# Unread matrix products in a tuned encoder layer: eight instead of two in the fourth feed-forward pair, one more ahead of three groups of gate pairs, and a wider one at the start

## The chip, the core and the metric

The kernel runs on one core of one Trainium2 chip. The time is what the device takes for one execution, in microseconds (us); the figure for a kernel is the median of its runs. The engines are called by the profile's names: PE is the matrix engine (TensorE), PEld its loading of weights, DVE is VectorE, ACT is ScalarE, POOL is GpSimd, SP is the queue that starts most transfers.

## What is computed

One layer of an encoder on 512 tokens of 1024 channels, all in float32. Cut to what matters here:

```
h      = rms_norm(x, norm1_g)
proj   = h @ w_in                       # 1024 x 7680: three mixers and three gates
y_*    = pool mixer, differential attention, gated recurrence (from slices of proj)
gates  = sigmoid(gate columns of proj)  # three branches x 1024 channels
merged = sum over branches of gates * (y_branch @ w_up_branch)
x      = x + merged @ w_out
h2     = rms_norm(x, norm2_g)
gu     = h2 @ w_ffn_in                  # 1024 x (2 x 2816): gate half, up half
x      = x + (silu(gate half) * up half) @ w_ffn_out
out    = rms_norm(x, final_norm_g)
```

## The kernel before

The tokens lie in four blocks of 128, the channels in eight tiles of 128. Every float32 matrix operand is split into a high part, cast to the rounded type that PE reads at one pass, and a low part, the remainder; a product is then three matmuls: high by high, high by low, low by high. The high part is cast on ACT (`whi`, line 183; `shi`, line 300), the low part subtracted on DVE (`wlo`, line 184; `slo`, line 302). A name such as `fhi`/`flo`, `ghi`/`glo`, `h_hi`/`h_lo`, `hT_hi`/`hT_lo` in a row of the profile is such a pair of the moving operand.

`Jobs.stream` (from line 223) walks through a list of jobs, and a job's matmuls are issued in the order in which the list stands; `tc.keep_in_program_order` holds PE to it. So PE's order is written out by hand, and DVE and ACT serve it.

Two stages use a seven-product scheme for a 2 x 2 block product, which takes seven block products where the plain way takes eight. In the feed-forward input a **pair** is one tile of 128 up columns and the tile of gate columns beside it; pairs 1 to 21 run this way, one after the other, in four jobs each (`first`, `second`, `third`, `fourth`, from line 1230). In the gates of the mixers, five pairs of gate tiles run this way (`gate_pair_bodies`, from line 653): one in the pool branch, two and two in the attention branch. Each pair is seven block products of 12 matmuls, 84 matmuls in all, each with 256 moving columns. The ups (`up_job`, from line 691) are products of a branch with its up weights, 12 matmuls of 512 columns per tile, two tiles from one weight part.

The kernel holds some operands at chosen distances in memory: `pad` puts 64 or 192 bytes ahead of a tile, and `skip` in `split_w` (line 178) moves the split weights by 64 or 192 bytes inside their buffer. In the gate pairs and in the feed-forward pairs the weights of a matmul start 64 bytes after its moving operand, if addresses are counted modulo 128; in most products with 512 columns they start at the same place. The part that two ups share ahead of a group of gate pairs has `skip=64`, which sets its weights 64 bytes off (`add_ups`, with `skips`, from line 726).

An **unread product** is a matmul whose result no instruction reads. In the fourth pair, `first` ends with two of them, which take the part's first weight tile and 512 columns of the same weights as the moving operand, the second one 16 elements (64 bytes) further on. They write to the PSUM name `tp`, which has two buffers. At the start, `busy(n)` issues n unread products of the 128 x 128 identity matrix with itself.

The program's order after the mixers is: pool ups and gates, the pool gate pair, ups, two attention gate pairs, ups, two attention gate pairs, ups, the output projection, the second norm, the feed-forward input (pairs 1 to 21), the feed-forward output.

Of the kernel before, what the change touches and what calls it, by code (L numbers as in the profile page):

```python
# [12 lines left out]
F32R = mybir.dt.float32r  # L13
# [5 lines left out]
P = 128  # L19
# [57 lines left out]
def encoder_kernel(ctx: ExitStack, tc: tile.TileContext, x, norm1_g, w_in, pool_w, pool_scale,  # L77
# [3 lines left out]
    nc = tc.nc  # L81
# [3 lines left out]
    def pool(name, bufs=1, **kw):  # L85
        return tc.tile_pool(name=name, bufs=bufs, **kw)


    def mm(out_, lhsT, rhs, start, stop, chain=False):
        i = nc.tensor.matmul(out_, lhsT=lhsT, rhs=rhs, start=start, stop=stop, skip_group_check=chain)  # L90
        tc.keep_in_program_order(i)
        n = 1
        for d in rhs.shape[1:]:
            n *= d
        pipe.t += max(0.107, n * 0.0004167 + 0.002) if rhs.dtype == F32R else max(0.216, n * 0.001667 + 0.004)
# [18 lines left out]
    def bank(name, shape=(P, 512)):  # L114
        return psum.tile(list(shape), F32, name=name, bufs=2 if name == "tp" else 3)
# [8 lines left out]
    ident = const.tile([P, P], F32, name="ident")  # L124
# [142 lines left out]
    @contextmanager  # L267
    def behind(after):

        with ExitStack() as st:  # L270
            for i in after:
                st.enter_context(tc.issue_after(i))
            yield
# [45 lines left out]
    def product(ps, part, n, r, start):  # L319

        terms = [(part.hi, r[0]), (part.hi, r[1]), (part.lo, r[0])]
        for i, (w, m) in enumerate(terms):
            for k in range(KT // 2):
                mm(ps, w[:, n, k, :], m[:, k, :], start and i == 0 and k == 0,
                   i == 2 and k == KT // 2 - 1, True)
                if k % 2:
                    yield
# [94 lines left out]
    def cols_mm(ps, part, r, nk, sub=0, lo_col=0, n=512, r_lo_last=False):  # L422
        c = slice(lo_col, lo_col + n)
        ws = slice(sub * P, sub * P + P)
        terms = [(part.hi, r[0]), (part.hi, r[1]), (part.lo, r[0])]
        if r_lo_last:
            terms[1:] = terms[:0:-1]
        for i, (w, m) in enumerate(terms):
            for k in range(nk):
                mm(ps[:, c], w[:, k, ws], m[:, k, c], i == 0 and k == 0, i == 2 and k == nk - 1)  # L430
                if k % 2:
                    yield
# [56 lines left out]
    xg = st0.enter_context(pool("xg"))  # L489
# [10 lines left out]
    for b in range(NB):  # L500
# [6 lines left out]
        if b >= 1:  # L507
            c = OFF[("rq", "rf", "rb")[b - 1]]
# [16 lines left out]
    def busy(n):  # L525

        ps = bank("mm")
        for _ in range(n):
            mm(ps[:, 0:P], ident, ident, True, True)
# [10 lines left out]
            transpose(gt[:, j, :], g_cols[:, half * 4 + j:half * 4 + j + 1].to_broadcast([P, P]), ident)  # L540
        nc.vector.tensor_copy(out=g_b[:, half * 512:half * 512 + 512], in_=gt.rearrange("p a b -> p (a b)"))

    busy(5)

    class First:
        wpool = None
# [144 lines left out]
    def up_job(idx, dt, y, first, last_hl):  # L691
        def body(part):
            ps = bank("mm")
            yield from cols_mm(ps, part, y(), 4, dt % 2)
            sg = gate_sb.pop((idx, dt))
            if first:
                nc.vector.tensor_tensor(out=merged[:, dt, :], in0=ps, in1=sg, op=ALU.mult)
                return
            nc.vector.tensor_tensor(out=sg, in0=ps, in1=sg, op=ALU.mult)
            nc.vector.tensor_tensor(out=merged[:, dt, :], in0=merged[:, dt, :], in1=sg, op=ALU.add)  # L700
            if last_hl:
                hi, lo = last_hl()
                nc.scalar.copy(out=hi[:, dt, :], in_=merged[:, dt, :])
                nc.vector.tensor_tensor(out=lo[:, dt, :], in0=merged[:, dt, :],
                                        in1=hi[:, dt, :].bitcast(F32), op=ALU.subtract)
        return body
# [479 lines left out]
    def ffn_pair_evac(j, pg, pu):  # L1186
        sl = FF["t"].tile([P, S], F32, name="silu")
        nc.scalar.activation(out=sl, in_=pg, func=AF.Silu)
        nc.vector.tensor_tensor(out=hid_of(j), in0=pu, in1=sl, op=ALU.mult)

    def hid_of(j):
        return FF["hid"][j // 8][:, j % 8, :]
# [33 lines left out]
    def ffn_pair_bodies(j):  # L1226
        c = {}


        def first(part):  # L1230
            f = FF["forms"]
            c["x"], c["zy"] = bank("mm")[:, 0:256], bank("rc")
            c["u"] = FF["t"].tile([P, S], F32, name="u")
            yield from product(c["x"], part, 0, f.r11, True)
            nc.scalar.copy(out=c["u"][:, 0:256], in_=c["x"])
            yield from product(c["zy"][:, 0:256], part, 1, f.r21, True)


            if j == 4:
                w = part.hi.rearrange("p n k c -> p (n k c)")  # L1240
                for skip in (0, 16):
                    mm(bank("tp"), w[:, 0:P], w[:, skip:skip + 512], True, True)

        def second(part):
            f = FF["forms"]
            y = c["y"] = c["zy"][:, 256:]
            if j == 2:
                with behind(FF["s12_2"]):
                    ffn_pair_evac(0, *FF["first"])
            c["g"] = FF["t"].tile([P, S // 2], F32, name="g2")  # L1250
            yield from product(c["x"], part, 1, f.n2, False)
            nc.scalar.copy(out=c["u"][:, 256:], in_=c["x"])
            yield from product(y, part, 0, f.n1, True)
            FF["y1"] = (nc.scalar.copy(out=c["g"], in_=y).ins,)

        def third(part):
            f = FF["forms"]
            if j == 1:
                with behind(FF["forms_end"]):
                    pairs[2][1].chunk.add()  # L1260
            c["sl"] = FF["t"].tile([P, S], F32, name="silu")
            yield from product(c["x"], part, 0, f.d, False)
            on_dve = nc.vector.tensor_tensor(out=c["g"], in0=c["x"], in1=c["g"], op=ALU.add).ins  # L1263
            if j == 1:
                FF["g1"] = (on_dve,)
            nc.scalar.activation(out=c["sl"][:, 256:], in_=c["g"], func=AF.Silu, scale=-1.0)
            yield from product(c["y"], part, 1, f.r22, False)
            nc.vector.tensor_tensor(out=c["u"], in0=c["u"], in1=c["zy"], op=ALU.add)

        def fourth(part):  # L1270
            f = FF["forms"]
            yield from product(c["x"], part, 0, f.n4, False)
            nc.scalar.activation(out=c["sl"][:, 0:256], in_=c["x"], func=AF.Silu, scale=-1.0)
            nc.vector.tensor_tensor(out=hid_of(j), in0=c["sl"], in1=c["u"], op=ALU.mult)
            if j == FT - 1:
                for i in range(2):
                    hid_split(i)

        return first, second, third, fourth

    pair_bodies = {j: ffn_pair_bodies(j) for j in range(1, FT)}
# [25 lines left out]
    def hid_split(i):  # L1307

        if i in hid_parts or i > LAST_JOB:
            return  # L1310
        hi, lo = (LAST["ws"].tile([P, 2, S], F32R, name=n) for n in ("shi", "slo"))
        j = PLAIN[i][0]
        view = FF["hid"][j // 8][:, j % 8:j % 8 + 2, :]
        nc.scalar.copy(out=hi, in_=view)
        nc.vector.tensor_tensor(out=lo, in0=view, in1=hi.bitcast(F32), op=ALU.subtract)
        hid_parts[i] = hi, lo
# [432 lines left out]
```

## Time and profile before

| | us |
|---|---|
| three runs | 891.97, 883.51, 885.41 |
| their median | 885.41 |
| the profiled execution, its own time | 892.81 |
| the profiled execution, its span | 891.0 |
| PE busy in it | 878.2 (99%) |
| DVE busy | 658.8 (74%) |
| ACT busy | 441.2 (50%) |

The span runs from the first to the last instruction that the profile holds; the execution's own time is 1.8 us longer, for what lies around it. The profiled execution is the longest of the four. A busy share of PE tells little here: matmuls overlap, so PE counts as busy also where each one takes longer than it could. What counts is the distance from the start of one matmul to the start of the next, and the timeline view gives it: its rows merge like instructions that follow each other, with the start of the first, the time until the last has ended, and their count.

### The profile page before, as it was taken

The numbers are of one execution on the slowest core, as the hardware profiler recorded it, in microseconds if no ns is written. First come the engines' busy times: TensorE is split into PE (matmuls) and PEld (weight loads), VectorE is DVE, ScalarE is ACT, GpSimd is POOL, SyncE is SP. The second block draws the span as 40 slices with busy tenths as digits, with TensorE's granted clock in tenths as the row PEclk, the third lists the DMA queues.
The fourth block names the chain that finished last, engine by engine and source line by source line (L and its number), as shares of the span: only waits on it lengthen the run. The fifth ranks groups of instructions, "written<-read, shape, count | busy, mean of one in ns | idle before, by whom it ended". The sixth has DMA issues, their size and how long they took to land.

```text
span 891.0 us, 13788 instructions
## 1 busy us (share of the span) xinstructions
PE 878.2 (99%) x5598; PEld 792.6 (89%) x5598; DVE 658.8 (74%) x992; ACT 441.2 (50%) x695; POOL 19.2 (2%) x35
## 2 busy tenths in 40 slices
PE   8999999999999999999999999999999999999996
PEld 7989988888988888888999898899999999988785
DVE  6788664845868764897785646988887888746996
ACT  5544343435656583443455335655555555433553
POOL 1000000000000000000000000000000000000001
PEclk9999999999999999999999999999999999999998
DMA  7330113024223123222331860344334432355002
GB/s 240 95 119 24 49 48 118 24 72 142 67 85 122 48 77 125 95 95 81 117 89 48 277 170 1 93 118 123 96 95 115 123 96 95 119 189 188 2 0 95
DMA packets 109579, 88.52 MB, mean 99 GB/s; under 512 B 2742, under 2 KB 98508, under 8 KB 109388
## 3 DMA queue, kind: packets, MB, share of 16 engines
q1 hardware_dynamic: 108924, 86.59, 31.6%
q8 instruction: 44, 0.72, 0.3%
q10 hardware_dynamic: 592, 1.05, 0.3%
q14 instruction: 19, 0.16, 0.1%
HBM read 85.54 MB, written 2.10 MB: 98 GB/s over the span
## 4 chain that ended last, share of the span: by engine, by line
PE 87%; DVE 6%; DMA 4%; issue 1%; ACT 1%; POOL 0%; SPq 0%; POOLq 0%; DVEq 0%; ACTq 0%
PE mm L90 60%; PE rc L90 23%; PE tp L90 2%; PE tp L98 2%; DMA raw<-in_w_out_dram 1%; DVE wlo L184 1%; DMA raw<-in_w_in_dram 1%; DMA raw<-in_w_ffn_out_dram 1%; DMA raw<-in_w_ffn_in_dram 1%; DVE hid L354 1%; DVE x L1323 0%; DMA xin<-in_x_dram 0%; DVE flo L354 0%; ACT whi L183 0%; DVE hrow L455 0%
## 5 line engine op out<-in xcount | busy, mean ns | idle before, releaser
L183 ACT CAST whi<-raw 128x1024 fp32r<-128x1024 f32 (+1 forms) x134 | 128.8, 967 | 147.4 <-PE mm L90 101.5
L184 DVE TENSOR_TENSOR wlo<-raw,whi 128x1024 fp32r<-128x1024 f32 (+1 forms) x134 | 149.0, 1118 | 54.1 <-ACT whi L183 34.3
L90 PE MATMUL mm<-hT_hi,wlo 128*128 128x512 f32 (+1 forms) x380 | 92.4, 375 | 0.2 <-DVE wlo L184 0.2
L90 PE MATMUL mm<-hT_hi,whi 128*128 128x512 f32 (+1 forms) x380 | 91.6, 376 | 0.0
L90 PE MATMUL mm<-hT_lo,whi 128*128 128x512 f32 (+1 forms) x380 | 90.7, 375 | 0.0
L90 PEld LDWEIGHTS mm<-hT_lo,whi 128*128 128x128 f32 x380 | 66.6, 189 | 11.5
L90 PEld LDWEIGHTS mm<-hT_hi,whi 128*128 128x128 f32 x380 | 66.4, 189 | 11.7 <-ACT hT_hi L468 0.4
L90 PEld LDWEIGHTS mm<-hT_hi,wlo 128*128 128x128 f32 x380 | 66.3, 188 | 11.6 <-DVE wlo L184 0.4
L302 DVE TENSOR_TENSOR slo<-sums,shi 128x1024 fp32r<-128x1024 f32 x52 | 63.3, 1218 | 0.1
L300 ACT CAST shi<-sums 128x1024 fp32r<-128x1024 f32 x52 | 54.6, 1051 | 3.8 <-DVE sums L264 2.3
L261 DVE TENSOR_TENSOR sums<-raw 128x1024 f32<-128x1024 f32 x26 | 31.7, 1220 | 3.5 <-DMA raw<-in_w_in_dram 3.5
L854 DVE TENSOR_TENSOR kq<-kq,pyr 128x256 f32<-128x256 f32 x48 | 18.2, 421 | 18.2 <-PE rc L90 18.2
L90 PE MATMUL rc<-kq,kc 128*128 128x128 f32 x224 | 31.6, 284 | 0.0
L90 PEld LDWEIGHTS rc<-kq,kc 128*128 128x128 f32 x224 | 30.1, 191 | 1.5
L996 ACT ACTIVATE s<-s,mx 128x512 f32<-128x512 f32 x32 | 23.0, 721 | 15.6 <-DVE mx L994 15.4
L1263 DVE TENSOR_TENSOR g<-mm,g 128x256 f32<-128x256 f32 x21 | 8.9, 424 | 28.4 <-PE mm L90 28.4
L823 ACT COPY kc<-kq 128x512 f32<-128x512 f32 x28 | 18.6, 666 | 20.3 <-PE rc L90 12.6
L90 PE MATMUL mm<-fhi,shi 128*128 128x256 f32 x168 | 26.7, 281 | 0.6 <-ACT shi L300 0.6
L90 PE MATMUL mm<-fhi,slo 128*128 128x256 f32 x168 | 26.9, 282 | 0.5 <-DVE slo L302 0.5
L90 PE MATMUL mm<-flo,shi 128*128 128x256 f32 x168 | 26.6, 281 | 0.0
L90 PE MATMUL mm<-y_hi,whi 128*128 128x512 f32 x96 | 26.6, 395 | 0.0
L90 PE MATMUL mm<-y_lo,whi 128*128 128x512 f32 x96 | 26.4, 393 | 0.0
(370 smaller groups left out, 1995.0 us busy)
## 6 DMA issues: line engine op xcount, KB each, us to landing
raw<-in_w_ffn_in_dram SPq DMA_DIRECT2D x44, 512.0 KB, 5.4
raw<-in_w_in_dram SPq DMA_DIRECT2D x34, 512.0 KB, 4.2
raw<-in_w_in_dram SPq DMA_DIRECT2D x13, 1024.0 KB, 5.3
raw<-in_w_ffn_out_dram SPq DMA_DIRECT2D x7, 1024.0 KB, 5.1
raw<-in_w_out_dram SPq DMA_DIRECT2D x4, 1024.0 KB, 9.8
xin<-in_x_dram SPq DMA_DIRECT2D x4, 512.0 KB, 4.7
raw<-in_w_up_rec_dram SPq DMA_DIRECT2D x2, 1024.0 KB
raw<-in_w_up_pool_dram SPq DMA_DIRECT2D x2, 1024.0 KB, 5.0
```

What stands on the lines that cost most here:

```text
L90: i = nc.tensor.matmul(out_, lhsT=lhsT, rhs=rhs, start=start, stop=stop, skip_group_check=chain)
L98: tc.keep_in_program_order(nc.tensor.transpose(out_, in_, idn))
L183: nc.scalar.copy(out=hi, in_=view)
L184: LAST["wlo"] = nc.vector.tensor_tensor(out=lo, in0=view, in1=hi.bitcast(F32), op=ALU.subtract).ins
L261: nc.vector.tensor_tensor(out=strided(sums, 0, [[2 * half, 2], [1, half]]), in0=strided(self.raw, 0, [[3 * half, 2], [1, half]]), in1=stri ...
L300: nc.scalar.copy(out=hi, in_=view)
L302: on_dve = nc.vector.tensor_tensor(out=lo, in0=view, in1=hi.bitcast(F32), op=ALU.subtract).ins
L354: last[0] = form(**kw).ins
L823: nc.scalar.copy(out=strided(kc, 0, [[2 * n, S // (2 * n)], [n, 2], [1, n]]), in_=strided(kq, 2 * S, [[2 * n, S // (2 * n)], [S + n, 2], [ ...
L854: nc.vector.tensor_tensor(out=xv, in0=xv, in1=tv, op=ALU.mult)
L996: nc.scalar.activation(out=s, in_=s, func=AF.Exp, scale=-1.0, bias=mx[:, c:c + 1], accum_out=zz[:, i, c:c + 1])
L1263: on_dve = nc.vector.tensor_tensor(out=c["g"], in0=c["x"], in1=c["g"], op=ALU.add).ins
```

## The change

Three edits.

1. At the start, five identity products of 128 columns are replaced by eleven products of 256 columns on a new tile `probe`, which ACT fills with eight copies of the identity. The weights are taken 48 elements (192 bytes) into the tile. The tile makes its pool 4 KB per partition larger; no operand of another matmul moves.
2. After the second tile of each part of ups that has `skip=64`, one unread product repeats the last matmul of that tile into `tp`. There are three such places: ahead of the pool gate pair, ahead of the first two attention gate pairs, and ahead of the last two.
3. In the fourth feed-forward pair eight unread products stand in place of two: six with the moving operand at the weights' own start, then two with it 48 elements (192 bytes) further on, which is 64 bytes modulo 128.

```
-    busy(5)
+    probe = xg.tile([P, 1024], F32R, name="probe")
+    nc.scalar.copy(out=probe, in_=ident.rearrange("p (o c) -> p o c", o=1).to_broadcast([P, 8, P]))
+    ps = bank("mm")
+    for _ in range(11):
+        mm(ps[:, 0:256], probe[:, 48:48 + P], probe[:, 0:256], True, True)
...
         def body(part):
             ps = bank("mm")
             yield from cols_mm(ps, part, y(), 4, dt % 2)
+            if part.skip and dt % 2:
+                mm(bank("tp"), part.lo[:, 3, P:2 * P], y()[0][:, 3, :], True, True)
...
             if j == 4:
                 w = part.hi.rearrange("p n k c -> p (n k c)")
-                for skip in (0, 16):
+                for skip in (0, 0, 0, 0, 0, 0, 48, 48):
                     mm(bank("tp"), w[:, 0:P], w[:, skip:skip + 512], True, True)
```

In PE's order of the changed program, the end of the fourth pair's first job looks as follows. `rc<-h_hi,wlo` is the last matmul group of that job, the rows with `tp<-whi` are the unread products, `mm<-fhi,shi` opens the second job; what stands in brackets is what a row's instructions wait for.

```order
L90 MATMUL rc<-h_lo,whi 128x256 x4
L90 MATMUL rc<-h_hi,wlo 128x256 x4
L90 MATMUL tp<-whi 128x512 x2
L90 MATMUL tp<-whi 128x512 [waits PE_49] x6
L90 MATMUL mm<-fhi,shi 128x256 [waits Activation_49]
L90 MATMUL mm<-fhi,shi 128x256 x3
```

The row with x6 is new. `tp` has two buffers, so from the third product on each one waits for PE's own semaphore, that is until the product two places ahead of it has ended.

At the third of the three places with ups, ahead of the last two attention gate pairs, PE's order changes thus; `y_hi` and `y_lo` are the branch's output, `hT_hi` opens the gate pair.

```order
 L90 MATMUL mm<-y_lo,whi 128x512 x4
 L90 MATMUL mm<-y_hi,wlo 128x512 x4
+L90 MATMUL tp<-y_hi,wlo 128x512 [waits PE_49]
 L90 MATMUL mm<-hT_hi,whi 128x256 [waits DVE_49]
 L90 MATMUL mm<-hT_hi,whi 128x256 x3
```

One matmul is put between the last up and the first gate product; nothing else changes its place. Its wait is for the first of the three added products, which has long ended (the gate pairs start at 424, 439 and 470 us).

## The prediction

> **What bounds the kernel now.** I read the page first: the busy time of the engines, and the chain of work that ended last.
>
> ```profile
> PE 878.2 (99%) x5598; PEld 792.6 (89%) x5598; DVE 658.8 (74%) x992; ACT 441.2 (50%) x695; POOL 19.2 (2%) x35
> ...
> PE 87%; DVE 6%; DMA 4%; issue 1%; ACT 1%; POOL 0%; SPq 0%; POOLq 0%; DVEq 0%; ACTq 0%
> ```
>
> PE is the chain for 87% of the span. An edit that adds matmuls is paid in full there, and one that changes the distance between matmuls by a few ns is paid, or earned, thousands of times. So the next view is the timeline of PE alone. At the end of the output projection stand three rows of eight matmuls with 256 columns, and the row after them:
>
> ```profile
> 521.57 1.07 PE L90 MATMUL mm<-whi,m_hi 128*128 128x256 f32 x8
> 522.48 1.07 PE L90 MATMUL mm<-whi,m_lo 128*128 128x256 f32 x8
> 523.39 1.07 PE L90 MATMUL mm<-wlo,m_hi 128*128 128x256 f32 x8
> 524.29 1.08 PE L90 MATMUL mm<-whi,m_hi 128*128 128x512 f32 x4
> ```
>
> From 521.57 to 524.29 are 2.72 us for 24 matmuls: 113.3 ns from start to start. In the feed-forward input the same shape, with the same distance of 64 bytes between weights and moving operand, goes more slowly. Here is the end of the fourth pair's first job, with the two unread products, and the end of the stage:
>
> ```profile
> 594.70 0.64 PE L90 MATMUL rc<-h_hi,wlo 128*128 128x256 f32 x4
> 595.17 0.62 PE L90 MATMUL tp<-whi 128*128 128x512 f32 x2
> 595.63 0.63 PE L90 MATMUL mm<-fhi,shi 128*128 128x256 f32 x4
> ...
> 770.88 0.39 PE L90 MATMUL mm<-whi,shi 128*128 128x512 f32 x1
> ```
>
> Between 595.63 and 770.88 stand the other five products of the fourth pair and 17 whole pairs: 5 x 12 + 17 x 84 = 1488 matmuls in 175.25 us, 117.8 ns each. So there are **two paces** for one shape, 113.3 and 117.8 ns. It isn't the clock, which is granted in full in the window from 600 to 640 us (the figure behind the busy times):
>
> ```profile
> core 0: us, PE busy (x) PEld busy (x) DVE busy (x) ACT busy (x) POOL busy (x), PEclk, DMA share, GB/s
> 600.00:640.00 40.00, 40.00 (x342) 40.00 (x341) 32.89 (x41) 21.97 (x36) 0.00 (x0) 1.00 0.39 107
> ```
>
> Nor does PE wait for anyone there (40.00 of 40). What sets the pace shows a little earlier, in pair 1, where both occur within 11 us on the same operands:
>
> ```profile
> 569.31 0.73 PE L90 MATMUL mm<-fhi,whi 128*128 128x256 f32 x4
> 569.88 0.62 PE L90 MATMUL mm<-flo,whi 128*128 128x256 f32 x4
> ...
> 573.06 0.62 PE L90 MATMUL rc<-h_hi,wlo 128*128 128x256 f32 x4
> 574.32 0.74 PE L90 MATMUL mm<-fhi,shi 128*128 128x256 f32 x4 [0.64 <-ACT shi L300]
> ...
> 579.04 0.74 PE L90 MATMUL mm<-fhi,slo 128*128 128x256 f32 x4 [0.46 <-DVE slo L302]
> 579.62 0.64 PE L90 MATMUL rc<-h_hi,shi 128*128 128x256 f32 x4
> ```
>
> The row at 569.31 takes 0.73 instead of 0.63 us: PE stopped for about 0.1 us. From 569.88 to 573.06 it then ran 28 matmuls in 3.18 us, 113.6 ns each: fast. The stop at 579.04 ended in the other pace, 0.64 us for four instead of 0.62, and so it stayed for all of the stage. A stop draws the pace anew; without one it stays. That explains the three runs as well. If the stretch behind the fourth pair ran fast, it would take 1488 x 4.5 = 6.6 us less. The runs of 891.97 and 885.41 lie 6.56 apart. I read them as this stretch slow, and fast; the profiled execution, with 892.81, is a slow one, and the median of 885.41 already has it fast.
>
> **The change part by part.** The sum is made against the profiled execution, 892.81.
>
> *The fourth pair, the products themselves.* Two are there now; from 595.17 to 595.63 they take 0.46 us. Eight would take 8 x 0.227 = 1.82 us (0.227 is half of 0.46, rounded down) if none waited. But from the third on each waits until the product two places ahead has ended, and no row of before has such a wait. For its price I use how long such a product lasts, and how long PEld needs behind an end:
>
> ```profile
> L90 PE MATMUL tp<-whi x2: 389/393/397, 595.2 to 595.4; 128*128 128x512 f32 x2
> ...
>   ACT whi L183: 1.5, 1
> ...
> 574.30 1.22 DVE L302 TENSOR_TENSOR slo<-sums,shi 128x1024 fp32r<-128x1024 f32 x1
> ...
> 575.57 0.53 PEld L90 LDWEIGHTS mm<-fhi,slo 128*128 128x128 f32 x4 [0.26 <-DVE slo L302]
> ```
>
> A product ends 0.39 us after its start. DVE ended at 575.52 and the waiting load began at 575.57: 0.05 us. The stopped rows above are 0.11 us longer than their neighbours, the load that is no longer hidden. Thus the third can start 0.39 + 0.05 + 0.11 = 0.55 us after the first, where it would come after 0.45. Going on like this, numbers 3, 5 and 7 start at 0.55, 1.10 and 1.65, each even one 0.23 behind, and the eighth ends its turn at 2.11 us. So the cost lies between 1.82 - 0.46 = **1.4** (no stop) and 2.11 - 0.46 = 1.65; I take **1.6**, near the upper end, since all its parts are measured rows. Below nothing it can't be: nothing else uses PE meanwhile. Queued behind the waiting products on PE is all of the stage. ACT's cast of the next weights waits for the last of them (1.5 us once, in the rows above); it comes later by what PE comes later, and ACT is busy for 22 of 40 us.
>
> *The fourth pair, the pace behind it.* The two products of before did not turn slow into fast in this execution. Six waits of fixed length stand there now; each is a stop, and of the two stops shown above one ended fast and one slow. Here the stop is PE's own, so it should end alike in every execution. Between **-6.6 us** (all 1488 fast) and nothing I take -6.6, because this place follows a stop as the fast row at 569.88 does. That DVE could become the bound in its place is excluded: 32.9 us in 40 become 32.9 in 38.5, 85%.
>
> *Ups ahead of the gate pairs.* Three more matmuls with 512 columns, not waiting for anything recent:
>
> ```profile
> 423.07 1.10 PE L90 MATMUL mm<-y_hi,wlo 128*128 128x512 f32 x4
> 424.01 0.64 PE L90 MATMUL mm<-hT_hi,whi 128*128 128x256 f32 x4
> ```
>
> Four take 0.94 us from 423.07 to 424.01, so three cost **+0.7**. The five gate pairs run slowly now: 0.64 for four, and all their matmuls on `ghi`, from the listing by groups, last 281 ns on average, against 276 in the fast output projection (the second row, of 505 to 524 us alone):
>
> ```profile
> L90 PE MATMUL mm<-ghi,slo 128*128 128x256 f32 x40 | 6.3, 281 | 0.0
> ...
> L90 PE MATMUL mm<-whi,m_lo 128*128 128x256 f32 x58 | 8.2, 276 | 0.0
> ```
>
> Fast, their 5 x 84 = 420 matmuls would take 420 x 4.5 = 1.9 us less. The run of 883.51 is 1.9 below that of 885.41, which I read as just that. One more matmul makes the number of ups odd, so the pair is entered at another place of whatever alternates. The bounds are -1.9 and nothing; I take **-1.9**, a little likelier than not, as that run shows the fast entry to exist.
>
> *The start.* ACT gets one more cast, of 128x1024, and PE eleven products of 256 columns for ten passes of 128:
>
> ```profile
> 4.52 1.06 ACT L449 ACTIVATE hrow<-xin 128x1024 f32<-128x1024 f32 x1 [2.31 <-DMA xin<-in_x_dram]
> ...
> 6.27 1.28 PE L90 MATMUL mm<-ident 128*128 128x128 f32 x10
> ...
> 7.65 0.66 PE L98 MATMUL tp<-ident,hrow 128*128 128x128 f32 x4
> ```
>
> ACT is idle for 2.31 us ahead of 4.52, and a cast of that size takes 0.97 us on average by the page's groups: hidden, else +1. Eleven products at 0.12 are 1.3 us from 6.27, to 7.57; the transposes start at 7.65, released by DVE. Between 0 and +0.3; I take **0**.
>
> The sum: 892.8 + 1.6 - 6.6 + 0.7 - 1.9 = **886.6 us**. That is 6.2 below the profiled execution, but 1.2 above the median, whose runs need no cure in the long stretch.
>
> **The rivals.**
>
> *The stop ends in the slow pace* (0.22 with the gate pairs slow too). For it: at 579.04 a stop did just that, and the two products of before left it slow. All additions are paid, nothing is earned: 892.8 + 1.6 + 0.7 = 895.1, slower than the median by 1.1%, in every run, since a fast entry would be lost as well. The point where it decides: the first matmul behind the eighth product. With the gate pairs fast it is 893.2 (0.10).
>
> *The long stretch fast, the gate pairs slow* (0.25): 886.6 + 1.9 = 888.5. For it: an odd number of products at that distance also stood ahead of 595.63 (one), and slow came of it.
>
> *The change doesn't do what it says* (0.05). The pace might not hang on these products at all, but on the stops before them. Then the draw stays as it was, two of three runs fast, and the median only gains the additions: 885.4 + 1.6 + 0.7 = 887.7. The Trainium skill speaks for this, in "TensorE: Matmul & The Clock Gate", section "Step-by-step: what each phase is for": "Loading the next tile's weights doesn't steal SBUF read bandwidth from the running matmul." By that rule no placing of weights could alter the pace, and the same page's gap of N/2.4 + 2.5 ns gives 109.2 for 256 columns always, an estimate. The trace disagrees: 113.3 and 117.8 for one shape at full clock. With the rule the sum would be the 887.7 just worked out; without it, the forecast.
>
> *The start is late* (0.03): the cast holds up ACT's first square, or the eleven products the transposes: up to +1.0 on the forecast, 887.6.
>
> **How the numbers follow.** Forecast, both fast: 0.35, 886.6 us. Others as given, 0.25, 0.22, 0.10, 0.05, 0.03. The cases with a fast long stretch span 886.3 to 888.5, and unprofiled runs lie 0.8 lower (891.97 for 892.81) and differ somewhat: from 884.5. The slow ones go to 895.1; they hold a third, so the range must take them in: 884.5 to 895.5. About 1% is what a measurement of this kernel can tell from no change, 876.6 to 894.3 here. Faster by that needs 9 us, more than every gain together: 0.02. Slower is the case of 895.1, which lies just beyond the bound, at 0.6 of its chance: 0.14. The same: 0.84.
>
> **What will show it.** In the changed profile: eight rows of `tp<-whi`, 2.1 us long with the third 0.55 behind the first (1.8, if nothing waits); behind them four matmuls in 0.62 rather than 0.64 us, up to the 512-column products, which start some 168.6 us later rather than 175.25; a mean of 276 rather than 281 for `mm<-ghi,slo`; the transposes on `hrow` at 7.65. I'd be wrong if stops behind the fourth pair draw the pace again, since DVE has less slack at the fast pace, or if earlier stops, which differ from run to run, move the time by more than this change does.

## The result, and the profile after

The changed kernel takes **891.89 us** in the median of 17 runs (891.47 to 893.02), the kernel before 885.41 in the median of 17 runs taken beside it (883.51 to 891.97). The ratio is 1.007 [1.0057, 1.0083]: within 1% of before, but slower. It is 6.5 us above the median of before and 5.3 above the forecast of 886.6. It lies inside the forecast's range of 884.5 to 895.5, which was wide enough to hold the slow rivals too, so the time alone says nothing for the forecast's mechanism.

The page of the changed kernel, busy time of the engines and the chain of work that ended last:

```profile
span 890.1 us, 13812 instructions
PE 878.3 (99%) x5608; PEld 792.8 (89%) x5608; DVE 658.7 (74%) x992; ACT 441.8 (50%) x696; POOL 19.8 (2%) x35
PE 91%; DVE 4%; DMA 2%; issue 1%; ACT 1%; POOL 0%; SPq 0%; POOLq 0%; DVEq 0%
```

PE is busy for the same 99%, and with 10 matmuls more it is busy 0.1 us longer: the page alone shows nothing. The timeline of PE around the fourth pair does (start, length, engine, line, operation, tiles, count). It starts at the last stop ahead of the products and ends at the first product with 512 columns behind the stage:

```profile
577.95 0.74 PE L90 MATMUL mm<-fhi,slo 128*128 128x256 f32 x4 [0.47 <-DVE slo L302]
578.52 0.62 PE L90 MATMUL rc<-h_hi,shi 128*128 128x256 f32 x4
...
593.04 0.62 PE L90 MATMUL rc<-h_hi,wlo 128*128 128x256 f32 x4
593.49 2.30 PE L90 MATMUL tp<-whi 128*128 128x512 f32 x8
595.63 0.64 PE L90 MATMUL mm<-fhi,shi 128*128 128x256 f32 x4
596.10 0.64 PE L90 MATMUL mm<-flo,shi 128*128 128x256 f32 x4
...
770.88 0.40 PE L90 MATMUL mm<-whi,shi 128*128 128x512 f32 x1
```

Four matmuls take 0.62 us from 578.52 on, up to the products: the pairs were entered in the fast pace. Behind the products four take 0.64, and 595.63 to 770.88 are 175.25 us for 1488 matmuls, 117.8 ns each, to the hundredth what the profiled execution of before had. **The eight products turn the fast pace into the slow one.** The window in which the prediction read 342 matmuls of before, here for PE alone:

```profile
core 0: us, PE busy (x), PEclk, DMA share, GB/s
600.00:640.00 40.00, 40.00 (x342) 1.00 0.38 104
```

The clock is granted in full, PE waits for nobody, and the count is that of the slow trace of before. (At 117.8 ns 340 matmuls fit in 40 us, at 113.3 ns 353; the view also counts the two or three that only reach into the window. So a slow trace shows 342, a fast one 355 or 356, and that count serves as the sign of the pace from here on.)

The products take 2.14 us, from 593.49 to 595.63. The weight loads (PEld) show how they wait:

```profile
593.38 0.30 PEld L90 LDWEIGHTS tp<-whi 128*128 128x128 f32 x2
593.94 0.42 PEld L90 LDWEIGHTS tp<-whi 128*128 128x128 f32 x2 [0.26 <-PE tp L90]
```

The third load waits for PE itself: the first product ended 0.39 us after 593.49, at 593.88, and the load began 0.06 later. In the version without waits, below, each load begins as the product ahead of it starts, which here would be 593.72.

The entry of the three groups of gate pairs, again in the timeline of PE: the last 512-column product ahead of each, and the first matmuls behind it.

```profile
424.04 0.40 PE L90 MATMUL tp<-y_hi,wlo 128*128 128x512 f32 x1
424.27 0.62 PE L90 MATMUL mm<-hT_hi,whi 128*128 128x256 f32 x4
...
439.39 0.39 PE L90 MATMUL tp<-y_hi,wlo 128*128 128x512 f32 x1
439.62 0.63 PE L90 MATMUL mm<-hT_hi,whi 128*128 128x256 f32 x4
440.09 0.64 PE L90 MATMUL mm<-hT_lo,whi 128*128 128x256 f32 x4
...
470.48 0.40 PE L90 MATMUL tp<-y_hi,wlo 128*128 128x512 f32 x1
470.71 0.62 PE L90 MATMUL mm<-hT_hi,whi 128*128 128x256 f32 x4
471.17 0.62 PE L90 MATMUL mm<-hT_lo,whi 128*128 128x256 f32 x4
```

The first and the third group became fast, the second stayed slow. That is 84 + 168 = 252 of the 420 matmuls, worth 252 x 4.5 = 1.1 us. The listing by groups has it as a mean between 281 and 276:

```profile
L90 PE MATMUL mm<-ghi,slo 128*128 128x256 f32 x40 | 6.2, 278 | 0.0
```

The start, which the prediction put at no cost (the transposes on `hrow` at 7.65):

```profile
6.36 1.54 PE L90 MATMUL mm<-probe 128*128 128x256 f32 x11
7.74 0.63 PE L98 MATMUL tp<-ident,hrow 128*128 128x128 f32 x4
```

### The profile page after: what moved, and what is told of

It reads as the page before. It is cut to its first block, busy times and chain, and to the rows that moved or that the text cites. A ratio compares the mean times of both kernels' runs of the same rounds, so it can differ in the third digit from the quotient of the medians.

```text
span 890.1 us, 13812 instructions
## 1 busy us (share of the span) xinstructions
PE 878.3 (99%) x5608; PEld 792.8 (89%) x5608; DVE 658.7 (74%) x992; ACT 441.8 (50%) x696; POOL 19.8 (2%) x35
## 4 chain that ended last, share of the span: by engine, by line
PE 91%; DVE 4%; DMA 2%; issue 1%; ACT 1%; POOL 0%; SPq 0%; POOLq 0%; DVEq 0%
PE mm L90 62%; PE rc L90 25%; PE tp L90 3%; PE tp L98 2%; DMA raw<-in_w_out_dram 1%; DMA raw<-in_w_in_dram 1%; DVE wlo L184 1%; DVE hid L354 1%; DVE flo L354 1%; DMA xin<-in_x_dram 0%; DVE hrow L455 0%; DVE h_lo L472 0%; PE rc L98 0%; DVE slo L302 0%; DVE sums L261 0%
```

## The experiments

The theory, called Theory 1 in the quoted expectations and T1 here: the last products ahead of a run of 256-column matmuls set the pace of that run, and the eight as built set the slow one. T1a is the form in which the distance of the last product from what follows decides, long or short, and the waits of the eight make them end on the short one. Against it stands that the pace is drawn at the stops ahead and that the products change nothing but their own length. Medians are in us; the kernel before ran beside each batch: 885.92 for the first four experiments, 886.21 for the next four, 885.09 for the last four. Over these batches 16 of its 85 runs lie above 889.5 us and the other 69 below 887.8, with nothing between 887.7 and 890.8. The three batches ran on three chips, and the high runs of before are spread unevenly over them: 3 of 25, 12 of 31 and 1 of 29.

**Two products again, all else changed.**

```
-                for skip in (0, 0, 0, 0, 0, 0, 48, 48):
+                for skip in (0, 16):
```

> The changed kernel with the two products of before in the fourth pair instead of the eight; the additions ahead of the gate pairs and at the start stay. Theory 1 (the eight products set the slow pace): the changed profile comes to them at 113.3 ns, and two products leave a fast pace as it is, so all 1488 matmuls behind them are fast: 891.9 - 6.6 (pace) - 1.7 (six products) = 883.6 us. Theory 2 (the pace behind is not set by the products; something after them makes it slow): only the six products are saved, 890.2 us, with 117.8 ns behind them.

884.02 (883.52 to 890.97), ratio 0.9983 [0.9962, 1.0005]. So the eight products carry the loss. The profiled execution happened to be the one of 890.97. Its timeline of PE:

```profile
593.78 0.63 PE L90 MATMUL rc<-h_hi,wlo 128*128 128x256 f32 x4
594.25 0.62 PE L90 MATMUL tp<-whi 128*128 128x512 f32 x2
594.71 0.63 PE L90 MATMUL mm<-fhi,shi 128*128 128x256 f32 x4
595.18 0.63 PE L90 MATMUL mm<-flo,shi 128*128 128x256 f32 x4
```

From 593.78 to 594.25 and from 594.71 to 595.18 are 0.47 us for four matmuls, 118 ns each: slow ahead, slow behind. Two products leave the pace as they find it: slow here and in the first trace of before, fast in the second trace of before, below.

**Eight products alone, in the kernel before.**

```
-                for skip in (0, 16):
+                for skip in (0, 0, 0, 0, 0, 0, 48, 48):
```

> The kernel before with the eight products in the fourth pair as its only edit. Theory 1: slow behind them in every run, 885.4 + 6.6 + 1.7 = 893.7 us. Theory 2 (the slow pace comes of the other two edits): 885.4 + 1.7 = 887.1 us, fast behind them.

895.16 (four runs: 893.18 and 895.02 to 895.40), ratio 1.0098 [1.0074, 1.0121]. The timeline of PE, and the window of 40 us, of the execution at 893.18:

```profile
594.33 0.62 PE L90 MATMUL rc<-h_hi,wlo 128*128 128x256 f32 x4
594.78 2.30 PE L90 MATMUL tp<-whi 128*128 128x512 f32 x8
...
600.00:640.00 40.00, 40.00 (x342) 1.00 0.38 106
```

Fast ahead of the products, slow behind them, as in the changed kernel. This speaks against T1a: by the starts in this trace the last of the eight took 238 ns, a long distance, and the pace behind it is slow all the same. The three runs without a profile are 1.3 to 1.7 us above the 893.7 that T1 gives; that is not explained.

**Eight products in one buffer: no waits between them.**

```
+                t = bank("tp")
                 for skip in (0, 0, 0, 0, 0, 0, 48, 48):
-                    mm(bank("tp"), w[:, 0:P], w[:, skip:skip + 512], True, True)
+                    mm(t, w[:, 0:P], w[:, skip:skip + 512], True, True)
```

> The changed kernel with its eight products written to one buffer of tp, so that none waits for an earlier one. Theory 1a (what counts is whether the last product with 512 columns ends in the long, 236 ns, or the short, 231 ns, one of the two distances that alternate): without waits the last two should take 225 and 236 ns, the pair is entered behind a long one, and all is fast: 891.9 - 6.6 - 0.3 (no waits) = 885.0 us. Theory 1b (any such row of products resets to slow): 891.6 us.

885.17 (884.59 to 885.92), ratio 0.9991 [0.9981, 1.0001]. The same eight products, and none of ten runs is slow. The timeline of PE, and the window:

```profile
593.63 2.00 PE L90 MATMUL tp<-whi 128*128 128x512 f32 x8
595.47 0.63 PE L90 MATMUL mm<-fhi,shi 128*128 128x256 f32 x4
595.94 0.62 PE L90 MATMUL mm<-flo,shi 128*128 128x256 f32 x4
...
600.00:640.00 40.00, 40.00 (x355) 1.00 0.41 114
```

They take 1.84 us instead of 2.14, so the waits themselves cost 0.3; the lost pace costs 6.6. The edit takes away two things together, the waits and the change from one buffer to the other with each product. No run parts them; what the traces show is that the distances of 316 to 336 ns of the waiting rows are gone (226 to 234 here). In one point the text above was wrong: the last two were to take 225 and 236 ns, and took 233 and 234.

**No products in the fourth pair at all** (the block `if j == 4:` removed).

> The changed kernel without any unread product in the fourth pair. Theory 1: the pace that the first three pairs reached goes on. It is fast in the changed profile (113.3 ns from 578.6 us), so 891.9 - 6.6 - 2.1 = 883.2 us. Theory 2: slow in the long stretch, 889.8 us. If the pace that pairs 1 to 3 reach differs from run to run, the runs fall into two groups 7 us apart.

883.61 (883.09 to 890.97, one run of ten above 884.3), ratio 0.9979 [0.9954, 1.0004]. Its window shows

```profile
600.00:640.00 40.00, 40.00 (x356) 1.00 0.43 116
```

By its trace, and by the times of nine runs of ten, the long stretch is fast without any product: what the stop ahead of it leaves. So the products of the changed kernel don't fail to set the fast pace, they destroy it.

**Is it the number of products?** Two, and three, in one buffer, with both operands 64 bytes apart:

```
+                t = bank("tp")
-                for skip in (0, 0, 0, 0, 0, 0, 48, 48):
-                    mm(bank("tp"), w[:, 0:P], w[:, skip:skip + 512], True, True)
+                for skip in (48, 48):               # and (48, 48, 48)
+                    mm(t, w[:, 0:P], w[:, skip:skip + 512], True, True)
```

> The changed kernel with two products in the fourth pair, both 64 bytes off, in one buffer without a wait. Theory of the alternation (a matmul with 256 columns goes on fast behind a long 512-column one, 235 or 236 ns, and slow behind a short one, 231; ahead of the second group of gate pairs a fast pair was followed by 226, 235, 231, 236 and so on): two products take 226 and 235, so all behind is fast, 883.6 + 0.1 = 883.7 us. Rival (only the settling by six products at the same start sets it, and two leave the entry as it is): also fast where the entry is fast, the same time; this run tells them apart only together with the next one.

> As the run before, with three such products. Theory of the alternation: the third is a short one, 231, and all behind it is slow: 883.7 + 0.2 + 6.6 = 890.5 us. Rival (products leave the entry as it is): fast, 883.9 us.

Two: 883.86 (883.06 to 885.57), ratio 0.9949 [0.9916, 0.9981]. Three: 890.35 (nine runs from 889.94 to 892.41, one at 883.94), ratio 1.0004 [0.9968, 1.0039] against a before with many high runs. One product of 0.23 us costs 6.5. All ten runs with two are low, beside 12 high runs of 31 for before on the same chip; drawn with that share, ten low ones in a row have a chance of under 1%. So two at this distance seem to set the fast pace, not only to leave it, but no trace shows them entered from the slow one. The timelines of PE, first with two, then with three:

```profile
595.45 0.62 PE L90 MATMUL tp<-whi 128*128 128x512 f32 x2
595.92 0.62 PE L90 MATMUL mm<-fhi,shi 128*128 128x256 f32 x4
```

```profile
592.78 0.62 PE L90 MATMUL rc<-h_hi,wlo 128*128 128x256 f32 x4
593.24 0.85 PE L90 MATMUL tp<-whi 128*128 128x512 f32 x3
...
595.34 0.64 PE L90 MATMUL rc<-fhi,shi 128*128 128x256 f32 x4
...
600.00:640.00 40.00, 40.00 (x342) 1.00 0.39 110
```

From start to start the two took 226 and 236 ns, the three 225, 236 and 231, both entered at 113 ns. The run of 883.94 has no profile; an entry in the slow pace, which the three would turn round, would fit it and was not seen.

**The second gate group, with no products in the fourth pair.** The group that stayed slow loses its added product:

```
-            if part.skip and dt % 2:
+            if part.skip and dt % 2 and (idx, dt) != (0, 7):
```

> The changed kernel without the products in the fourth pair and without the one added ahead of the second group of gate pairs; those ahead of the first and third group stay. Theory of the alternation: entered from a fast pair, 24 ups there end long, and the group of 168 is fast as the other two are: 883.6 - 0.2 (one product less) - 0.75 (168 x 4.45 ns) = 882.7 us. Rival (it takes an added product to become fast): slow there as before, 883.4 us; the trace tells.

882.89 (seven runs from 882.49 to 882.94, three from 890.55 to 892.15), ratio 0.9956 [0.9914, 0.9998]. The listing by groups:

```profile
L90 PE MATMUL mm<-ghi,slo 128*128 128x256 f32 x40 | 6.2, 276 | 0.0
```

276, the mean of the fast output projection: all three groups are fast. By the starts the last 512-column product ahead of the second group now took 236 ns, with the added one it had been 231. But three runs of ten end 7.7 to 9.3 us higher. A slow pace from the last stop on, over 132 + 1488 = 1620 matmuls, would be 1620 x 4.5 = 7.3 of it, and nothing in the fourth pair is there to mend one; these runs have no profile.

**Can a slow stretch be turned back?** Eight products in one buffer once more, in the eighth pair of the changed kernel:

```
+            if j == 8:
+                w = part.hi.rearrange("p n k c -> p (n k c)")
+                t = bank("tp")
+                for skip in (0, 0, 0, 0, 0, 0, 48, 48):
+                    mm(t, w[:, 0:P], w[:, skip:skip + 512], True, True)
```

> The changed kernel, which runs slowly behind its eight waiting products in the fourth pair, with eight more in the eighth pair, to one buffer and so without a wait, as in the experiment with one buffer. If such a row sets the fast pace whatever it is entered with: slow up to the eighth pair, fast for the 60 + 13 x 84 = 1152 matmuls behind it, 891.9 + 1.8 - 5.1 = 888.6 us. If it only keeps a fast entry: slow to the end, 893.7 us.

889.53 (888.11 to 890.22), ratio 1.0009 [0.9978, 1.004]. Yes. The windows ahead of them and behind:

```profile
600.00:640.00 40.00, 40.00 (x336) 1.00 0.35 97
680.00:720.00 40.00, 40.00 (x355) 1.00 0.43 119
```

The first window holds the second set itself, as the timeline of PE shows:

```profile
634.76 1.99 PE L90 MATMUL tp<-whi 128*128 128x512 f32 x8
636.59 0.63 PE L90 MATMUL mm<-fhi,shi 128*128 128x256 f32 x4
```

So its 336 is not a count of the slow pace alone. By the starts, the 336 matmuls between the two sets follow each other at 117.8 ns, the 1152 behind the second set at 113.3. The same loop runs ahead of the second set and behind it, so the pace is a state, and a row of products without waits leaves it fast: coming from slow here, from fast in the experiment with one buffer. The median is 0.9 above the 888.6 expected; that is left open.

**The other two edits alone, in the kernel before.** The added product ahead of the gate pairs (`if part.skip and dt % 2:` and its `mm`), and the eleven products on `probe` in place of `busy(5)`:

> The kernel before with the three products ahead of the gate pairs as its only edit. Theory of the alternation: the first and the third group become fast (84 + 168 matmuls), the second stays slow since it is now entered from a fast pair: 0.7 - 252 x 0.00445 = -0.4 us against the kernel before where both run the long stretch at the same pace, so 885.0 to 885.8 us. Rival of the prediction (all three become fast): -1.2 us.

> The kernel before with the eleven wider products at the start as its only edit. All theories: nothing on the path, so within 0.3 us of the kernel before where both run the long stretch at the same pace; the transposes at 7.7 us, the gate pairs slow as before.

884.44 (883.70 to 891.92), ratio 0.9991 [0.9968, 1.0014], and 885.33 (884.61 to 885.98), ratio 0.9994 [0.9977, 1.001]. Neither does anything that can be told from nothing; the first lies 0.6 below the 885.0 to 885.8 expected, and its trace is of the run of 891.92, with the long stretch slow. In the trace of the first the gate groups one and three are fast and two slow, as in the changed kernel; in the second all are slow, and the transposes start at 7.57 rather than 7.65.

**The kernel before, once more with a profile.**

> The kernel before, for a second trace of it. If the draw is as read from its times, most likely a run of 884 to 886 us with the stretch behind the fourth pair at 113.3 ns, its two products entered from a fast pace and left in it, and all three groups of gate pairs slow.

886.06. Its window shows, against the 342 of its first profiled execution,

```profile
600.00:640.00 40.00, 40.00 (x355) 1.00 0.43 120
```

By the starts, its matmuls come to the two products at 113.3 ns, the two take 232 ns each, and the 1488 behind them go on at 113.3. Both paces occur in one program, run to run, and 886.06 and 892.81 are what they give.

**All gate groups fast, six products in one buffer.** The condition of the second-group experiment, and

```
+                t = bank("tp")
-                for skip in (0, 0, 0, 0, 0, 0, 48, 48):
-                    mm(bank("tp"), w[:, 0:P], w[:, skip:skip + 512], True, True)
+                for skip in (0, 0, 0, 0, 48, 48):
+                    mm(t, w[:, 0:P], w[:, skip:skip + 512], True, True)
```

> The changed kernel without the product ahead of the second group of gate pairs, and with six products to one buffer in the fourth pair, four at the weights' own start and two 64 bytes off. Theory: all gate pairs fast, as in the run without the second product, and the long stretch fast in every run, whatever pace the stops ahead of it drew: 882.9 + 6 x 0.228 = 884.3 us with no run near 891. Rival (four do not settle it as six did): some runs 6.6 us longer, as without products.

884.16 (twelve runs, 883.32 to 885.21), ratio 0.9984 [0.9969, 1.0000]. Its timeline of PE:

```profile
592.55 1.55 PE L90 MATMUL tp<-whi 128*128 128x512 f32 x6
593.94 0.63 PE L90 MATMUL mm<-fhi,shi 128*128 128x256 f32 x4
594.40 0.62 PE L90 MATMUL mm<-flo,shi 128*128 128x256 f32 x4
```

0.9 below the median of before, at the edge of what the runs can tell, and 7.7 below the changed kernel, which ran in another batch. No run of twelve is high, but with 1 of 29 for before on this chip that says little by itself. With the other two versions whose products stand in one buffer and end fast (eight, and two) it makes 32 runs without a high one, of which the ten with two, beside 12 of 31, weigh most. Where nothing sets the pace (before, the change with two products or none, the second-group version, the gate edit and the start edit alone) 24 of 153 are above 889.5.

## Why the prediction was right or wrong

**The two paces: right.** In every trace the 1488 matmuls of the long stretch, or the 336 and 1152 parts of it, go at 113.3 or at 117.8 ns, at a granted clock of 1.00, and the two traces of before, 886.06 and 892.81, have it fast and slow.

**The pace behind the fourth pair: wrong, and this is the step that failed.** The prediction took -6.6, "because this place follows a stop as the fast row at 569.88 does"; measured is 0 against the profiled execution, since both are slow in all 1488 matmuls. Against the median it is +6.6: the stretch was fast in most runs of before, and by their times, 891.47 to 893.02, it is slow in all 17 of the changed kernel. "The stop is PE's own, so it should end alike in every execution" was right; in which pace, a row about another stop could not tell. The rival "The stop ends in the slow pace" has it, with its place (the first matmul behind the eighth product), its mechanism ("a fast entry would be lost as well"), and, of the two times it names, 895.1 with the gate pairs slow and 893.2 with them fast, the nearer to 891.89 is 1.3 above it. That the way in which the eight are built makes the end slow is shown by the same eight products in one buffer: 885.17, fast. Whether it is their waits or the change of buffers stays open, and so does what in PE the pace is.

That 891.89 lies in the forecast's range is luck as far as the forecast's mechanism goes: the range was drawn so wide for the rivals, and one of them came.

What misled was the choice of the execution against which the sum was made. It was one of the rarer slow ones, in which the products had nothing to lose. Seen from a fast one, the same question reads: will the products keep what is there? Only one of the two ends of the range is then a loss, and it is the whole 6.6.

**The eight products: right in their sum.** Predicted 2.11 us from the first to what follows, measured 2.14; over the 0.46 of the two that is +1.7 for +1.6. (Half of 0.46 is 0.23 rather than the 0.227 used; the eight without waits, in one buffer, took 1.84 for the 1.82.) The third's load begins 0.06 us behind the first's end, against 0.05, and ACT's cast of the next weights waits for the products 3.1 us instead of 1.5, which costs PE nothing in the 1488 matmuls. In the trace the delay isn't where the text has it, though: the timeline shows the third 0.47 behind the first, with 0.48 instead of 0.39 for its length, and the fourth start late:

```profile
593.96 0.48 PE L90 MATMUL tp<-whi 128*128 128x512 f32 x1
```

```profile
594.28 0.72 PE L90 MATMUL tp<-whi 128*128 128x512 f32 x2
```

**Products ahead of the gate pairs, and their pace: half right.** Three products cost 3 x 0.23 = 0.7. Of the -1.9 only -1.1 came, from groups one and three. What decides is visible to a nanosecond in the starts: ahead of these two the last product took 236 ns, ahead of the second group 231. The products there take 231 and 236 in turn, so one more turns the entry round, but the second group comes out of another entry than the other two. Taking its product away again made that group fast. The reading of the run at 883.51 as one with fast gate pairs is not borne out: in both traces of before they are slow, and that run has none.

**The start: right.** The transposes come at 7.74 instead of 7.65, and the edit alone gives 885.33 against 885.09.

**The sum.** With the measured terms, against the profiled execution: 892.8 + 1.7 + 0 + 0.7 - 1.1 = 894.1 for 891.9. Of the 2.2 left, 132 matmuls ahead of the products that were fast this time (578.52 to 593.49) make 0.6, and a stop in the next stage about 0.8. It stands in the timeline of before, and not in that of the changed kernel:

```profile
843.76 0.73 PE L90 MATMUL mm<-h_hi,whi 128*128 128x512 f32 x2
844.90 0.73 PE L90 MATMUL mm<-h_hi,whi 128*128 128x512 f32 x2 [0.40 <-DVE h_hi L1407]
```

```profile
843.63 1.07 PE L90 MATMUL mm<-h_hi,whi 128*128 128x512 f32 x4
844.54 0.62 PE L90 MATMUL mm<-shi,whi 128*128 128x512 f32 x2
```

Of the remaining 0.8, about 0.2 is fast matmuls in the pairs ahead of the stops of pair 1, and the rest waits of other lengths, by the two traces' starts. None of this was tested.

## What to carry to other kernels

Where one shape shows two paces at full clock, treat the pace as a state: find what sets it, and who could lose it, before pricing an edit by what it could win. Make the sum against the kind of execution that the median comes from, and where the runs fall into two groups, take a profile of each. Where unread work is to set such a state, try it without waits for itself: here the same eight products in one buffer cost 0.3 us less and left the fast pace, while through two buffers, with waits, the runs were slow every time.

## What the runs showed of the hardware

- The pace depends on what ran before, not on the two operands' addresses alone: one program, the kernel before, ran the same 1488 matmuls at 117.8 ns in one execution and at 113.3 in another. With 64 bytes between weights and moving operand, products with 512 columns take 231 and 236 ns in turn; behind one of 236 the 256-column matmuls ran at 113.3 ns (gate groups one and three, and the version with two), behind one of 231 or 229 at 117.8 (the second group, the version with three, and the changed kernel). It is not a full rule: the eight in one buffer ended with 233 and 234, and fast; the two of before took 227 and 236 from slow and left it slow, 232 and 232 from fast and left it fast; and the eight with waits, alone in the kernel before, ended with 238, and slow.
- The Trainium skill, in "TensorE: Matmul & The Clock Gate", section "Step-by-step: what each phase is for", was cited ahead of the result for weight loads that take no read bandwidth from the running matmul. From it the prediction drew that the pace should be one and the same; the measurement decides against that: here one load and product more moved all 1488 matmuls behind it from 113.3 to 117.8 ns (883.86 against 890.35). Whether read bandwidth is what the slow pace lacks, no run here shows.
- In the changed kernel each of the six loads that wait for a product on their own engine began 0.06 us behind that product's end, and with two buffers a pair of 512-column products then took 0.55 to 0.57 us instead of 0.46.
